# A decoder block on one core: a fourth slot for raw weights in three stages, and seven-product steps placed later in two blocks

## The chip, the core and the metric

The kernel runs on one core of one Trainium2 chip. The core has a matrix engine (PE, with its weight loads shown as PEld), VectorE (DVE), ScalarE (ACT), GpSimd (POOL) and SyncE (SP), which work through their own instruction queues and wait for one another by semaphores. Here SP issues nearly all loads of weights, and POOL issues the transfers that add to what they find in SBUF. The metric is the time of one execution on the device in microseconds (us). The kernel before takes 1745.06 us, the median of three runs (1744.52 to 1749.61).

## The reference, cut to what matters

One layer of a decoder over 256 tokens of width 2048 in float32. The weights are read once and make up nearly all of the transfers.

```python
a = rmsnorm(h, norm_mix_pre)
proj = a @ w_in                               # 2048 x 17408
q_a, k_a, v_a, q_r, f_r, i_r, g_r, gate_a, gate_r = split_columns(proj)
# attention in three dilated groups, and a gated linear recurrence (HGRN2)
y = sigmoid(gate_a) * (attn @ w_attn_branch) + sigmoid(gate_r) * (r_out @ w_hgrn_branch)
h = h + rmsnorm(y @ w_mix_out, norm_mix_post)
a = rmsnorm(h, norm_ffn_pre)
gt, up = split(a @ w_ffn_gate_up)             # 2048 x 11264
ff = (silu(gt) * up) @ w_ffn_down             # 5632 x 2048
h = h + rmsnorm(ff, norm_ffn_post)
```

## The kernel before, in words

**Products.** To keep float32 accuracy, each operand is split into a high and a low part of the type fp32r, and a product is three matmuls: high by high, high by low, low by high. ACT writes the high part of the weights (`w`, L368) and DVE the low part (`wl`, L381), both from the tile `raw` in which the float32 weights arrived.

**Blocks and steps.** The work is a list of blocks (`blocks`), each made of steps (`seq`). A block of the class `Wide` makes 1024 columns in two groups of 512 for all 256 tokens. One of its steps takes 256 rows of the weights, so 1 MB, and multiplies a 2 x 2 arrangement of tokens (two halves of 128) and rows (two of 128) by a 2 x 2 arrangement of rows and column groups. There are two kinds. An **eight-step** makes the eight products plainly, with 24 matmuls of 128 x 512. A **seven-step** makes seven products by a Strassen scheme, with 21 matmuls. For that it needs sums of weights: a transfer that POOL issues (L296) adds 256 KB to the first quarter of `raw`, once the load of that half has landed; DVE makes `sum` from `raw` (L375, L376), ACT its high part `dh` (L386) and DVE its low part `dl` (L389). It also needs sums of activations, made ahead.

**Where they stand.** Tables of strings say which step of a block is which: `EARLY` for eight blocks over `w_in` (gates, values and the recurrence's input), `FFN` for ten blocks over `w_ffn_gate_up`, `DOWN` for two over `w_ffn_down`; `MIX` for two over `w_mix_out`. Most blocks of `EARLY` and `FFN` read "87878787". In time: two narrow blocks, the early wide blocks from about 52 to 405 us, other blocks with the attention and the recurrence beside them to about 940, the mix, two narrow FFN blocks, the FFN blocks to about 1500, and the down blocks to the end.

**Slots.** The tile `raw` has `N_RAW` = 3 slots. The unit of loading is a wide step (or two narrow ones). `load_behind` is called when a step has been split, and asks for the unit three further on, whose slot is the one that the split has just read for the last time. The loads stand in SP's queue in that order, and each waits for its slot's readers.

**What stands beside a step.** While step n is being multiplied, `ahead(n)` prepares step n+2: ACT's high part, the sums where it is a seven-step, DVE's low part; and `dh` and `dl` of step n+1. `sum`, `dh` and `dl` have one buffer each, `w` and `wl` three.

**Block ends.** A wide block holds four PSUM banks (two pairs) for its outputs and four for the products that several outputs share. The next block takes them the other way round. `gather` (L451 to L454) brings the shared products into the tile `e` after the block's last seven-step: ACT copies the first (L451), DVE adds the others. `add_up` (L463) then adds the outputs. The early blocks go on with a sigmoid or a copy (L735) and a store of `e` by POOL's queue (L736); the FFN blocks with silu (L1389), a product (L1391), and a transposition on PE (L1355) inside the next block's second step. Where a block closes with a seven-step, the sums of the step after next stand ahead of the gather in DVE's queue, and its low part behind it.

**Between mix and FFN**, `from_mix_to_ffn` writes an order by hand. It splits three units early; the third has no free slot of `w` and is split into the tile `sum` (`sumslot`).

The lines that decide all this:

```python
EARLY = [order(x) for x in ["88787878"] + ["87878787"] * 6 + ["88787878"]]
FFN = [order(x) for x in ["88787878"] + ["87878787"] * 8 + ["87878787"]]
N_RAW, N_SPLIT, AHEAD, WARM, BRIDGE, LATER = 3, 3, 2, 8, 6, 16
```

Of the kernel before, what the change touches and what calls it, by code (L numbers as in the profile page):

```python
# [39 lines left out]
def order(steps):  # L40

    k = steps.count("7")
    return [(steps[:i].count(x) + k * (x == "8"), int(x == "7")) for i, x in enumerate(steps)]


EARLY = [order(x) for x in ["88787878"] + ["87878787"] * 6 + ["88787878"]]
FFN = [order(x) for x in ["88787878"] + ["87878787"] * 8 + ["87878787"]]
DOWN = [[(m, m in by7) for m in range(KF // 2)] for by7 in (range(4, 20, 3), range(3, 19, 3))]

TURN = 1  # L50
# [54 lines left out]
def tile_hybrid_block(ctx: ExitStack, tc: tile.TileContext, t, out):  # L105
# [12 lines left out]
    def nm(s):  # L118
        serial[0] += 1
        return f"{s}_{serial[0]}"  # L120
# [63 lines left out]
        )  # L184


    warm = cpool.tile([P, 512], mybir.dt.bfloat16, name="warm")
    nc.vector.memset(warm, 0.0)
    ones = cpool.tile([P, P], F32R, name="ones")
    ident = cpool.tile([P, P], F32, name="ident")  # L190
    make_identity(nc, ident)
    nc.gpsimd.tensor_scalar(ones, ident, 0.0, 1.0, op0=OP.mult, op1=OP.add)
    eps = cpool.tile([P, 2], F32, name="eps")
    nc.gpsimd.memset(eps[:, 0:1], EPS)
    nc.gpsimd.memset(eps[:, 1:2], -0.5 * EPS)
    rowg = cpool.tile([48, P], F32, name="rowg")
    nc.scalar.dma_start(rowg[0:16], t["norm_mix_pre"][0].rearrange("(a p) -> a p", p=P))
    nc.scalar.preload_act_table_set("natural_log_exp_and_others")
    colg = cpool.tile([P, 56], F32, name="colg")
    r1c = cpool.tile([P, 2], F32, name="r1c")  # L200
    rzc = cpool.tile([P, 2], F32, name="rzc")
    r2c = cpool.tile([P, 2], F32, name="r2c")
    r3c = cpool.tile([P, 2], F32, name="r3c")
    rowb = cpool.tile([P, S], F32, name="rowb")

    stage = ctx.enter_context(ExitStack())
    pool = {}

# [12 lines left out]
    kp = stage.enter_context(tc.tile_pool(name="kp", bufs=1, reuse_waits="tile"))  # L221
    enter("early")

    def fslot(s):
        return pool["now"].tile([P, 1024], F32, tag="f", bufs=16, name=nm(s))

# [9 lines left out]
    masks = {}  # L236


    blocks, seq, units = [], [], []

    def add(*args, **kw):
        b = Block(*args, **kw)
# [6 lines left out]

    def add_seven(*args, flip, whole=True, **kw):  # L250
        b = Wide(*args, **kw)
        b.flip, b.whole = flip, whole
# [23 lines left out]
    def load(u, half):  # L276

        if u >= len(units) or half >= len(units[u]):
            return
        st = units[u][half]  # L280
        b, i = st.block, st.i
        if half == 0:
            raw = stream.tile([P, 2048], F32, tag="raw", bufs=N_RAW, name=nm("raw"))
            for x in units[u]:
                x.raw = raw
        if type(b) is Wide:
            m, by7 = b.order[i]
# [12 lines left out]
        src = b.w[i * rows : (i + 1) * rows, b.col : b.col + b.width]  # L300
        src = src.rearrange("(k p) c -> p k c", p=P)
        dst = st.raw.rearrange("p (k c) -> p k c", k=b.per)
        n = len(parts(st))
        for x in range(n):
            ks = slice(x * b.per // n, (x + 1) * b.per // n)
            nc.sync.dma_start(dst[:, ks, :], src[:, ks, :])

    def load_behind(st):

        for half in (0, 1) if len(units[st.unit]) == 1 else (st.half,):  # L310
            load(st.unit + N_RAW, half)

    def wslot():
        return stream.tile([P, 2048], F32R, tag="w", bufs=N_SPLIT, name=nm("w"))

    def sumslot():
        return p3("sum", F32R, 2048, 1)

    def wlow():
        return p3("wl", F32R, 2048, 3)  # L320
# [1 line left out]
    def split(st, only=None):  # L322
# [3 lines left out]
        raw = st.raw  # L326
        if st.parts is None:
            w = (st.home or wslot)()
            st.parts = w[:, :1024], w[:, 1024:]
        wh, wl = st.parts  # L330
        for n, k in enumerate(parts(st)):
            if only in (None, n):
# [895 lines left out]
    def from_mix_to_ffn(n):  # L1228
# [4 lines left out]

        b, c, f0, f1, f2 = seq[n : n + 5]
        m = b.block
        f1.home, f2.home = wlow, sumslot
        split(f2)
        split(f0)
        load_behind(f0)
# [300 lines left out]
    mix_end = len(seq) - 2  # L1540
    w = t["w_ffn_gate_up"][0]
    add("N", w, KD, 0, lambda k: hT[0](k), evac_first_gate,
        post=more_h)
# [158 lines left out]
```

## Time and profile before

| | us |
|---|---|
| median of three runs | 1745.06 |
| the profiled execution | 1745.72 |
| its span, first to last instruction | 1743.9 |
| ACT busy, early wide blocks (353 us) | 185.8 |
| DVE idle before the first sum (L375), early wide blocks, until a load of `w_in` has landed | 37.7 |
| ACT idle before `w` (L368), FFN blocks, until a load of `w_ffn_gate_up` has landed | 101.5 |

How to read it: the page gives for each engine the time in which it worked and its share of the span. A window is a stretch of the span with each engine's busy time in it and, in brackets, how many instructions. A wait is idle time of an engine, put down to the instruction or transfer whose end released it. The chain goes back from the last instruction to what released it, step by step. In the timeline a row shows start, duration, engine, line and tiles, and in square brackets the idle time ahead of it and what ended it. Matmuls overlap in the records, so their spacing and not their duration is the rate.

### The profile page before, as it was taken

To read this page: it belongs to the slowest core of one execution; us is meant where nothing else is said; L and a number is where in the kernel's file an instruction comes from. 1 tells how busy PE (TensorE), PEld (TensorE's weight loads), DVE (VectorE), ACT (ScalarE), POOL (GpSimd) and SP (SyncE) were. 2 spreads that over 40 slices of the span, in tenths; PEclk is the share of its full clock that TensorE was granted. 3 is DMA by queue.
4 is the path that set the end of the run, shared out by engine and by line. 5 is a ranking of instruction groups with operands and counts; after the bars stand their busy time and mean duration, and the time that the engine had idled before them with its cause. 6 is when DMAs were issued, how large, how long until landed. Compare 5 with 4: busy or idle time off the path is not lost.

```text
span 1743.9 us, 21581 instructions
## 1 busy us (share of the span) xinstructions
PE 1695.9 (97%) x8220; PEld 1414.6 (81%) x8220; DVE 1416.8 (81%) x1443; ACT 914.8 (52%) x943; POOL 105.3 (6%) x141
## 2 busy tenths in 40 slices
PE   9999899999999999999999999999999999999998
PEld 7787777788888888888888888877777777888886
DVE  6888788886787987777678888888888888898887
ACT  6555455454544433544445575555555455665663
POOL 0111110111000000000000000000000000000000
PEclk9999999999999999999999999999999999999999
DMA  8787777778554655465458747776777777777663
GB/s 284 220 255 239 219 239 240 234 229 282 188 165 161 206 181 181 158 217 172 155 179 262 253 129 240 224 208 202 213 210 215 213 207 209 225 236 227 209 211 124
DMA packets 218600, 367.07 MB, mean 210 GB/s; under 512 B 12064, under 2 KB 78672, under 8 KB 218496
## 3 DMA queue, kind: packets, MB, share of 16 engines
q1 hardware_dynamic: 198208, 317.89, 55.2%
q0 software_dynamic: 17664, 41.89, 11.4%
q10 hardware_dynamic: 2624, 5.92, 1.0%
q8 instruction: 64, 1.05, 0.2%
q14 instruction: 40, 0.33, 0.1%
HBM read 354.12 MB, written 11.53 MB: 210 GB/s over the span
## 4 chain that ended last, share of the span: by engine, by line
PE 54%; DMA 16%; DVE 10%; issue 3%; ACT 2%; POOLq 0%; DVEq 0%; SPq 0%; ACTq 0%
PE acc L164 39%; PE aux L164 14%; DMA raw<-in_w_ffn_gate_up 12%; DVE wl L381 4%; DMA raw<-in_w_in 4%; ACT w L368 1%; DVE e L463 1%; DVE dl L389 1%; DVE e L454 1%; DVE sum L376 1%; DVE e L1391 0%; DVE e L452 0%; PE aux L889 0%; DVE e L453 0%; DVE sum L375 0%
## 5 line engine op out<-in xcount | busy, mean ns | idle before, releaser
L368 ACT ACTIVATE w<-raw 128x2048 fp32r<-128x2048 f32 x204 | 390.1, 1912 | 360.7 <-DMA raw<-in_w_ffn_gate_up 103.3
L381 DVE TENSOR_TENSOR wl<-raw,w 128x2048 fp32r<-128x2048 f32 x204 | 466.5, 2287 | 31.1 <-ACT w L368 28.1
L164 PE MATMUL acc<-xT,w 128*128 128x256 f32 (+1 forms) x2048 | 369.8, 339 | 0.0
L164 PEld LDWEIGHTS acc<-xT,w 128*128 128x128 f32 x2048 | 312.0, 188 | 43.8
L334 DVE TENSOR_TENSOR w<-raw,w 128x1024 fp32r<-128x1024 f32 (+1 forms) x191 | 232.5, 1218 | 133.0 <-ACT w L333 131.9
L333 ACT ACTIVATE w<-raw 128x1024 fp32r<-128x1024 f32 (+1 forms) x191 | 200.8, 1053 | 224.5 <-PE acc L164 179.4
L386 ACT ACTIVATE dh<-sum 128x1536 fp32r<-128x1536 f32 x85 | 126.5, 1488 | 92.5 <-DVE sum L376 67.3
L164 PE MATMUL acc<-w,hT 128*128 128x512 f32 x566 | 170.1, 392 | 5.0 <-DVE e L452 5.0
L164 PE MATMUL acc<-w,xT 128*128 128x512 f32 x524 | 157.2, 397 | 7.2 <-DVE e L452 6.9
L389 DVE TENSOR_TENSOR dl<-sum,dh 128x1536 fp32r<-128x1536 f32 x85 | 148.9, 1752 | 3.0 <-ACT dh L386 3.0
L375 DVE TENSOR_TENSOR sum<-raw 128x512 f32<-128x512 f32 x85 | 58.5, 688 | 114.1 <-issue 44.1
L164 PE MATMUL aux<-w,hT 128*128 128x512 f32 x414 | 137.8, 397 | 8.7 <-DVE e L452 8.7
L164 PEld LDWEIGHTS acc<-w,hT 128*128 128x128 f32 x566 | 105.7, 188 | 28.5 <-DVE e L452 6.7
L164 PEld LDWEIGHTS acc<-w,xT 128*128 128x128 f32 x524 | 98.8, 190 | 29.5 <-DVE e L452 7.8
L164 PE MATMUL aux<-w,xT 128*128 128x512 f32 x332 | 110.4, 398 | 6.6 <-DVE e L452 6.6
L376 DVE TENSOR_TENSOR sum<-raw,sum 128x1024 f32<-128x1024 f32 x85 | 104.1, 1225 | 2.9
L164 PEld LDWEIGHTS aux<-w,hT 128*128 128x128 f32 x414 | 79.2, 191 | 27.1 <-DVE e L452 10.4
L164 PE MATMUL aux<-w,a 128*128 128x512 f32 x280 | 88.6, 389 | 0.0
L164 PE MATMUL acc<-w,a 128*128 128x512 f32 x280 | 88.3, 389 | 0.0
L164 PE MATMUL acc<-wl,hT 128*128 128x512 f32 x211 | 81.3, 393 | 3.6 <-DVE wl L381 3.6
L164 PE MATMUL aux<-wl,hT 128*128 128x512 f32 x207 | 82.0, 396 | 1.5 <-DVE wl L381 1.5
L164 PEld LDWEIGHTS aux<-w,xT 128*128 128x128 f32 x332 | 63.7, 192 | 21.2 <-DVE e L452 7.8
(284 smaller groups left out, 2620.2 us busy)
## 6 DMA issues: line engine op xcount, KB each, us to landing
raw<-in_w_in SPq DMA_DIRECT2D x271, 512.0 KB, 4.7
raw<-in_w_ffn_gate_up SPq DMA_DIRECT2D x176, 512.0 KB, 4.7
raw<-in_w_ffn_down SPq DMA_DIRECT2D x88, 512.0 KB, 5.1
raw<-in_w_mix_out SPq DMA_DIRECT2D x32, 512.0 KB, 5.6
raw<-in_w_ffn_gate_up POOLq DMA_DIRECT2D x39, 256.0 KB, 4.4
kept<-e POOLq DMA_DIRECT2D x16, 512.0 KB, 4.9
raw<-in_w_hgrn_branch SPq DMA_DIRECT2D x16, 512.0 KB, 4.4
raw<-in_w_attn_branch SPq DMA_DIRECT2D x16, 512.0 KB, 4.4
```

The costliest lines, as they stand in the source:

```text
L164: nc.tensor.matmul(ps, lhsT, rhs, start=start, stop=stop, skip_group_check=True)
L333: nc.scalar.activation(wh[:, k], raw[:, k], AF.Copy)
L334: nc.vector.tensor_sub(wl[:, k], raw[:, k], wh[:, k].bitcast(F32))
L368: nc.scalar.activation(hi, raw, AF.Copy)
L375: nc.vector.tensor_sub(d[:, 0], w[:, 0], w[:, 2])
L376: nc.vector.tensor_sub(d[:, 1:], w[:, 1:4:2], d[:, 0:1].to_broadcast([P, 2, 512]))
L381: nc.vector.tensor_sub(lo, raw, hi.bitcast(F32))
L386: nc.scalar.activation(hi, flat, AF.Copy)
L389: nc.vector.tensor_sub(lo, flat, hi.bitcast(F32))
L454: nc.vector.tensor_sub(e[:, 2:], e[:, 0:4:3], x["p7"][:, None, :].to_broadcast([P, 2, 512]))
L463: nc.vector.tensor_add(e, b.bank[keys], e)
```

## The change

It has two parts and what makes room for them.

1. **A fourth slot.** A new tile `raw` with one buffer is taken from the pool of the stage (`p3`), beside the three slots of the pool `stream`. Lists of units in `extra` say which units use it: every fourth one, from the fourth of the early wide blocks to the last of them, and again from the fifth unit of the FFN wide blocks to the end. While such a list runs, `load_behind` asks for the unit four further on instead of three; where a list begins, it asks for one unit more, and where it ends, it asks for none.
2. **Steps placed later.** The first early block reads "88878878" instead of "88787878": two seven-steps instead of three, the fourth and the seventh step. The first FFN block reads "88878787": three as before, the fourth, sixth and eighth step, so that it closes with one.
3. **Room.** The small tile `rowg` moves to the pool of the early stage, which is opened earlier in the program for it, and the third unit between mix and FFN is split into the tiles `dh` and `dl` instead of `sum`, which shrinks from 2048 to 1536 elements a partition.

```diff
-EARLY = [order(x) for x in ["88787878"] + ["87878787"] * 6 + ["88787878"]]
-FFN = [order(x) for x in ["88787878"] + ["87878787"] * 8 + ["87878787"]]
+EARLY = [order(x) for x in ["88878878"] + ["87878787"] * 6 + ["88787878"]]
+FFN = [order(x) for x in ["88878787"] + ["87878787"] * 8 + ["87878787"]]
...
-    rowg = cpool.tile([48, P], F32, name="rowg")
+    rowg = pool["now"].tile([48, P], F32, name="rowg")
...
-            raw = stream.tile([P, 2048], F32, tag="raw", bufs=N_RAW, name=nm("raw"))
+            raw = raw_slot(u)
...
+    def raw_slot(u):
+        if any(u in x for x in extra):
+            return p3("raw", F32, 2048, 1)
+        return stream.tile([P, 2048], F32, tag="raw", bufs=N_RAW, name=nm("raw"))
+
     def load_behind(st):
 
-        for half in (0, 1) if len(units[st.unit]) == 1 else (st.half,):
-            load(st.unit + N_RAW, half)
+        u, depth, more = st.unit, N_RAW, None
+        for x in extra:
+            if u == x[0] - N_RAW - 1:
+                more = x[0]
+            if x[0] - N_RAW <= u < x[-1]:
+                depth = N_RAW + 1
+            elif u == x[-1]:
+                return
+        for half in (0, 1) if len(units[u]) == 1 else (st.half,):
+            load(u + depth, half)
+            if more:
+                load(more, half)
...
-    def sumslot():
-        return p3("sum", F32R, 2048, 1)
+    def sums_home():
+        return [p3(x, F32R, 1536, 1)[:, :1024] for x in ("dh", "dl")]
...
-            st.parts = w[:, :1024], w[:, 1024:]
+            st.parts = w if type(w) is list else (w[:, :1024], w[:, 1024:])
...
-        f1.home, f2.home = wlow, sumslot
+        f1.home, f2.home = wlow, sums_home
...
+    wide = [st.unit for st in seq if type(st.block) is Wide]
+    extra.append(range(wide[0] + N_RAW, wide[0] + 64, N_RAW + 1))
+    first = blocks[mix_last + 3].unit0 + N_RAW + 1
+    extra.append(range(first, len(units) + N_RAW + 1, N_RAW + 1))
```

How it moves instructions, at three places. First POOL's queue at the end of the first and of the second early block. `raw` with its numbers is a unit's tile of weights, `kept<-e` the store of a block's result. Before:

```order
L296 DMA raw_139_850<-in_w_in 128x512
L736 DMA kept_145_914<-e_140_875 128x1024 x2
L296 DMA raw_150_929<-in_w_in 128x512
L296 DMA raw_163_1000<-in_w_in 128x512
L296 DMA raw_172_1067<-in_w_in 128x512
L296 DMA raw_181_1138<-in_w_in 128x512
L736 DMA kept_186_1198<-e_185_1193 128x1024 x2
```

and with the change:

```order
L296 DMA raw_142_885<-in_w_in 128x512
L751 DMA kept_143_913<-e_138_873 128x1024 x2
L296 DMA raw_154_964<-in_w_in 128x512
L296 DMA raw_165_1033<-in_w_in 128x512
L296 DMA raw_174_1104<-in_w_in 128x512
L296 DMA raw_185_1200<-in_w_in 128x512
L751 DMA kept_184_1196<-e_183_1191 128x1024 x2
```

Four adding transfers lie between two pairs of stores in both. But the last one ahead of the second pair, `raw_181`, belongs to the fourth step of the third block, and `raw_185` to that block's sixth: the transfer for the sixth step has moved ahead of the stores of the block before.

Second, DVE's queue in the first early block. `wl` is the low part of a step's weights, `sum` and `dl` belong to a seven-step; `f`, `s` and `so` are sums of activations, `g` a gate of the block before. Before, from the second step's `wl` on:

```order
L381 TENSOR_TENSOR wl_588<-raw_468,w_587 128x2048
L479 TENSOR_TENSOR so_562<-s_563,so_562 128x512
L375 TENSOR_TENSOR sum_619<-raw_525 128x512
L376 TENSOR_TENSOR sum_619<-raw_525,sum_619 128x1024
L381 TENSOR_TENSOR wl_617<-raw_525,w_616 128x2048
L486 TENSOR_TENSOR f_656<-xT_109 128x512
L473 TENSOR_TENSOR s_659<-f_656 128x256
L474 TENSOR_TENSOR s_659<-s_659,f_656 128x128
L475 TENSOR_TENSOR s_659<-f_656,s_659 128x128
L389 TENSOR_TENSOR dl_664<-sum_619,dh_663 128x1536
L381 TENSOR_TENSOR wl_667<-raw_571,w_666 128x2048
```

and with the change:

```order
L396 TENSOR_TENSOR wl_591<-raw_468,w_590 128x2048
L494 TENSOR_TENSOR so_565<-s_566,so_565 128x512
L396 TENSOR_TENSOR wl_619<-raw_525,w_618 128x2048
L501 TENSOR_TENSOR f_656<-xT_109 128x512
L488 TENSOR_TENSOR s_659<-f_656 128x256
L489 TENSOR_TENSOR s_659<-s_659,f_656 128x128
L490 TENSOR_TENSOR s_659<-f_656,s_659 128x128
L390 TENSOR_TENSOR sum_666<-raw_528 128x512
L391 TENSOR_TENSOR sum_666<-raw_528,sum_666 128x1024
L396 TENSOR_TENSOR wl_664<-raw_528,w_663 128x2048
```

The two sums have moved from the third step's weights (`raw_525`) to the fourth's (`raw_528`), behind the sums of activations, and one set of `sum` and `dl` less stands in the block.

Third, DVE's queue at the end of the first FFN block, around its gather (into `e`). Before:

```order
L389 TENSOR_TENSOR dl_8628<-sum_8598,dh_8627 128x1536
L381 TENSOR_TENSOR wl_8631<-raw_8534,w_8630 128x2048
L381 TENSOR_TENSOR wl_8663<-raw_8568,w_8662 128x2048
L452 TENSOR_TENSOR e_8691<-acc_8543,e_8691 128x512
L453 TENSOR_TENSOR e_8691<-acc_8550,e_8691 128x512
L454 TENSOR_TENSOR e_8691<-e_8691,acc_8550 128x1024
L375 TENSOR_TENSOR sum_8699<-raw_8602 128x512
L376 TENSOR_TENSOR sum_8699<-raw_8602,sum_8699 128x1024
L381 TENSOR_TENSOR wl_8697<-raw_8602,w_8696 128x2048
L463 TENSOR_TENSOR e_8691<-aux_8450,e_8691 128x1024
```

and with the change:

```order
L404 TENSOR_TENSOR dl_8659<-sum_8629,dh_8658 128x1536
L396 TENSOR_TENSOR wl_8662<-raw_8530,w_8661 128x2048
L390 TENSOR_TENSOR sum_8696<-raw_8564 128x512
L391 TENSOR_TENSOR sum_8696<-raw_8564,sum_8696 128x1024
L467 TENSOR_TENSOR e_8720<-acc_8574,e_8720 128x512
L468 TENSOR_TENSOR e_8720<-acc_8581,e_8720 128x512
L469 TENSOR_TENSOR e_8720<-e_8720,acc_8581 128x1024
L478 TENSOR_TENSOR e_8720<-aux_8446,e_8720 128x1024
L478 TENSOR_TENSOR e_8720<-aux_8459,e_8720 128x1024
L396 TENSOR_TENSOR wl_8694<-raw_8564,w_8693 128x2048
```

The sums for the next block's second step now stand ahead of the gather, and that step's `wl` behind both adds of L463 (L478 in the changed file), as at the ends of the other FFN blocks.

More of the change, by code (lines that the diff above doesn't have):

```diff
@@ L184, in rsqrt_mean @@
         )
[L187 to L195, printed above, removed]
-    rowg = cpool.tile([48, P], F32, name="rowg")
[L197 to L204, printed above, removed]
     stage = ctx.enter_context(ExitStack())
@@ L222, in tile_hybrid_block @@
     enter("early")
+    warm = cpool.tile([P, 512], mybir.dt.bfloat16, name="warm")
+    nc.vector.memset(warm, 0.0)
+    ones = cpool.tile([P, P], F32R, name="ones")
+    ident = cpool.tile([P, P], F32, name="ident")
+    make_identity(nc, ident)
+    nc.gpsimd.tensor_scalar(ones, ident, 0.0, 1.0, op0=OP.mult, op1=OP.add)
+    eps = cpool.tile([P, 2], F32, name="eps")
+    nc.gpsimd.memset(eps[:, 0:1], EPS)
+    nc.gpsimd.memset(eps[:, 1:2], -0.5 * EPS)
+    rowg = pool["now"].tile([48, P], F32, name="rowg")
+    nc.scalar.dma_start(rowg[0:16], t["norm_mix_pre"][0].rearrange("(a p) -> a p", p=P))
+    nc.scalar.preload_act_table_set("natural_log_exp_and_others")
+    colg = cpool.tile([P, 56], F32, name="colg")
+    r1c = cpool.tile([P, 2], F32, name="r1c")
+    rzc = cpool.tile([P, 2], F32, name="rzc")
+    r2c = cpool.tile([P, 2], F32, name="r2c")
+    r3c = cpool.tile([P, 2], F32, name="r3c")
+    rowb = cpool.tile([P, S], F32, name="rowb")
     def fslot(s):
@@ L236, in tile_hybrid_block @@
     masks = {}
-    blocks, seq, units = [], [], []
+    blocks, seq, units, extra = [], [], [], []
     def add(*args, **kw):
@@ L251, in add_seven @@
         b = Wide(*args, **kw)
-        b.flip, b.whole = flip, whole
+        b.flip, b.whole, b.unit0 = flip, whole, len(units)
         blocks.append(b)
@@ L1540, in tile_hybrid_block @@
     mix_end = len(seq) - 2
+    mix_last = len(blocks) - 1
     w = t["w_ffn_gate_up"][0]
```

## The prediction

> **What bounds the kernel now.** The page first: the matrix engine (PE) has work 97% of the span, yet only about half of the chain that ended last is PE; the rest is transfers and VectorE (DVE).
>
> ```profile
> span 1743.9 us, 21581 instructions
> ...
> PE 1695.9 (97%) x8220; PEld 1414.6 (81%) x8220; DVE 1416.8 (81%) x1443; ACT 914.8 (52%) x943; POOL 105.3 (6%) x141
> ...
> PE 54%; DMA 16%; DVE 10%; issue 3%; ACT 2%; POOLq 0%; DVEq 0%; SPq 0%; ACTq 0%
> ```
>
> A busy share averages over stages, so next the windows: the early wide blocks (52 to 405 us), the FFN wide blocks (1100 to 1500), the down blocks (1503 to 1700), and one stretch of 50 us. Behind PE's busy time stand its instructions in brackets; the last three columns are the granted PE clock, the share of the transfer engines and GB/s.
>
> ```profile
> 52.00:405.00 353.00, 333.99 (x1433) 271.75 (x1433) 291.65 (x208) 185.77 (x122) 35.43 (x47) 0.98 0.77 235
> 1100.00:1500.00 400.00, 381.11 (x1684) 310.14 (x1683) 339.04 (x231) 213.76 (x146) 29.90 (x35) 0.99 0.72 210
> 1503.00:1700.00 197.00, 197.00 (x875) 163.26 (x874) 175.13 (x166) 119.12 (x110) 10.27 (x12) 1.00 0.71 220
> ...
> 1100.00:1150.00 50.00, 48.14 (x210) 39.37 (x209) 41.44 (x29) 28.46 (x21) 4.25 (x5) 0.97 0.68 195
> ```
>
> The down blocks never wait. The chain gives their undisturbed rate, and the timeline the length of a group of eight transposes:
>
> ```profile
> 1529.90 12.92 PE aux L164 x57
> ...
> 1108.25 1.03 PE L1355 MATMUL aux<-ident,e 128*128 128x128 f32 x8
> ```
>
> 12.92/57 = 0.2267 us a product. An eight-step (24 matmuls) is then 5.44 us and a seven-step (21) 4.76. The lost time of a stage is its length less its instructions at this rate. Early: 353 - 1433 x 0.2267 = **28.2 us**. FFN: nine groups of transposes (72 instructions, 9 x 1.03 = 9.3 us) are among the 1684; 400 - 1612 x 0.2267 - 9.3 = **25.3 us**. Control: the down stretch gives 197 - 875 x 0.2267 = -1.4, so the method is good to 1%. Together 53.5 us are lost in the two stages, and nothing that the change touches is lost elsewhere.
>
> Whom PE waits for, early and then FFN:
>
> ```profile
> PE acc L164 <- DVE e L452: 6.9, 2, 5.2
> PE aux L164 <- DVE e L452: 6.6, 3, 3.4
> PE acc L164 <- DVE wl L381: 2.2, 2, 1.5
> PE acc L164 <- DVE dl L389: 1.7, 2, 1.0
> PE aux L164 <- DVE wl L381: 1.6, 3, 0.8
> ...
> PE aux L164 <- DVE e L452: 8.7, 4, 2.8
> PE acc L164 <- DVE e L452: 5.0, 4, 1.6
> PE acc L164 <- DVE wl L381: 3.6, 5, 0.8
> PE aux L164 <- DVE wl L381: 1.5, 2, 0.7
> ```
>
> 19.0 and 18.8 us of waits, mostly for L452, the add that empties the PSUM pair a block left behind; the next block's first product needs that pair. The rest of the 53.5 is restart after a wait and the clock: the 50 us stretch above holds one wait of 50 - 48.14 = 1.9 us and a mean granted clock of 0.97, which is 1.5 us more. The Trainium skill ("TensorE: Matmul & The Clock Gate", Part 1) has the clock fall only after a whole idle window of about 3.4 us; the trace disagrees, since it fell around 1.9. By that page the FFN would lose little beyond its 18.8 of waits, and some 6 us less could be won; the measurement decides.
>
> Why is L452 late? The chain around one such boundary:
>
> ```profile
> 1128.92 1.42 DVE wl L381
> ...
> 1130.36 3.91 DMA raw<-in_w_ffn_gate_up
> ...
> 1135.09 6.10 DMA raw<-in_w_ffn_gate_up
> ...
> 1141.33 1.92 ACT w L368
> ...
> 1143.76 0.70 DVE e L452
> ```
>
> The last reader of a raw slot (wl, L381) ends at 1130.34; the load goes into it; a seven-step's adding transfer on POOL's queue (L296) may start only when that has landed; at 1141.18 the unit is whole. That is **10.8 us from free slot to usable weights**. ScalarE's (ACT) split and DVE's sums stand ahead of L452 in their queues, so L452 waits for weights that are not its own. DVE around it:
>
> ```profile
> 1141.27 0.69 DVE L375 TENSOR_TENSOR sum<-raw 128x512 f32<-128x512 f32 x1 [3.00 <-DMA raw<-in_w_ffn_gate_up]
> 1141.99 1.23 DVE L376 TENSOR_TENSOR sum<-raw,sum 128x1024 f32<-128x1024 f32 x1
> 1143.76 0.69 DVE L452 TENSOR_TENSOR e<-aux,e 128x512 f32<-128x512 f32 x1 [0.55 <-ACT e L451]
> ...
> 1145.29 1.22 DVE L454 TENSOR_TENSOR e<-e,aux 128x1024 f32<-128x1024 f32 x1
> 1146.61 2.35 DVE L463 TENSOR_TENSOR e<-acc,e 128x1024 f32<-128x1024 f32 x2
> 1148.88 2.28 DVE L381 TENSOR_TENSOR wl<-raw,w 128x2048 fp32r<-128x2048 f32 x1
> 1151.08 1.22 DVE L1391 TENSOR_TENSOR e<-e 128x1024 f32<-128x1024 f32 x1
> 1152.22 1.75 DVE L389 TENSOR_TENSOR dl<-sum,dh 128x1536 fp32r<-128x1536 f32 x1
> ...
> 1188.85 0.69 DVE L452 TENSOR_TENSOR e<-acc,e 128x512 f32<-128x512 f32 x1 [0.55 <-ACT e L451]
> ```
>
> DVE's only large idle time in the FFN is at L375 (two rows), and early it is the same place (third row):
>
> ```profile
> DVE sum L375 <- issue: 30.9, 10, 5.0
> DVE sum L375 <- DMA raw<-in_w_ffn_gate_up: 19.6, 7, 3.7
> ...
> DVE sum L375 <- DMA raw<-in_w_in: 37.7, 10, 5.3
> ```
>
> **The fourth slot.** With three slots, unit u+3 is loaded once u is split. Between that wl and the sums of u+3 DVE itself runs sums (1.9), wl (2.2), dl (1.7), wl (2.2): 8.0 us, start to start from the rows above. The weights take 10.8: 2.8 short, and the row of L375 shows 3.00. With four slots u+4 is loaded, a seven-step's load follows a seven-step's wl, and at PE's pace there lie two pairs of steps less one sums-and-wl: 2 x (5.44 + 4.76) - 4.1 = 16.3 us. The shortage of 2.8 becomes a reserve of **5.5**. Then the waits at L375 go, and with them the cause of the L452 waits.
>
> What is late next? DVE's own work: per FFN block 4 x 8.0 for the steps plus 2.8 (gather, L452 to L454), 2.3 (L463) and 1.1 (L1391) is 38.2 us against PE's 4 x (5.44 + 4.76) + 1.0 = 41.8. It fits, at 91%. At the boundary, counted from the start T of a closing seven-step with weights in time: ACT's split waits for PE's step before and ends at T+2.1, the copy L451 takes 0.55 (the wait in L452's row), L452 runs T+2.65 to T+3.35, and PE wants its pair at T+4.76: 1.4 us early. The wl of step 1 ends 7.4 us after L452 starts (1143.76 to 1151.16 above), at T+10.05; PE wants it at T+4.76+5.44+0.23 = T+10.43. That margin is only 0.4 us, dl's about 0.5. So each boundary costs between 0 and half of the present 25.3/9 = 2.8 us, that is 1.4. I take **0.3**, near the lower end since each margin comes out positive: with 16 boundaries 4.8 us stay.
>
> Queues: the extra load ahead of the first early wide block waits for no slot, and ahead of the second FFN step only for users of earlier stages; each later load stands in SP's order where a load stood. POOL's adding transfer of a block's sixth step now stands ahead of the two stores of the block before (L736). It waits for its load, so the stores go out at about T+15 (step 1's wl at T+10.05 and one landing) and no longer soon after L463's end at T+7.9: at most 7 us later. Behind the stores only the next adding transfers wait, and the tile e is next written a block later, 41 us off. So 0; without those 41 us of cover it would be the 7 us once per early block.
>
> **The steps placed later.** The first early block has two seven-steps instead of three: 24 - 21 = 3 more matmuls, 3 x 0.2267 = **+0.7 us** on PE. Its two dl waits (1.7 us above) should go, being part of the 28.2; the wait of at most 0.8 us for the first wl stays, since DVE there still works on the block before. The first FFN block keeps three, shifted by one, and now closes with one, which makes its boundary like the others (counted in the 16). There PE waited for nothing, so the bounds are 0 and 1.4; I take the 0.3 included. Splitting the third unit between stages into dh and dl instead of sum has the same two instructions; the ACT write already follows a split waiting for the same PE step: 0. Moving rowg and the fourth slot behind the down blocks: PE never waits there, 0.
>
> **Sum**, against the profiled execution's 1745.72 us (span 1743.9 and 1.8 around it; the median shown is 1745.06, 0.7 less): 1745.7 - 53.5 + 0.8 + 4.8 + 0.7 = 1698.5; from the median 1697.8. I say **1698**.
>
> **Rivals.** *Transfers become the bound early.* The stretch at 235 GB/s moved 353 x 235 = 83 MB; in 353 - 28.2 + 5 = 330 us that is 252 GB/s.
>
> ```profile
> GB/s 284 220 255 239 219 239 240 234 229 282 188 165 161 206 181 181 158 217 172 155 179 262 253 129 240 224 208 202 213 210 215 213 207 209 225 236 227 209 211 124
> ...
> 400.00:450.00 50.00, 48.64 (x265) 41.98 (x266) 34.55 (x39) 25.11 (x30) 6.05 (x9) 1.00 0.82 267
> ...
> raw<-in_w_in SPq DMA_DIRECT2D x120, 512.0 KB, 5.4
> raw<-in_w_in POOLq DMA_DIRECT2D x29, 256.0 KB, 4.3
> ...
> raw<-in_w_ffn_gate_up SPq DMA_DIRECT2D x128, 512.0 KB, 4.8
> ```
>
> For it: few slices exceed 252. Against it: 50 us at 267 and a slice at 284 exist, and the share would be 0.77 x 252/235 = 0.83, as in that window. If half the early loss stays: 14.1 instead of about 3, hence 1709. Chance 0.13.
>
> *DVE becomes the bound at the boundaries.* The margins of 0.4 and 0.5 us may be negative. At 1.4 instead of 0.3 a boundary: 16 x 1.1 = 17.6 more, 1716. For it: DVE at 91% with an in-order queue; against it: the worked times. Chance 0.16.
>
> *It doesn't reach the cause.* If POOL's transfer stays late for another reason than the slot, DVE waits as now: 1746. The chain, in which slot, load and transfer follow without a gap, speaks against. Chance 0.05.
>
> *Slower.* The adding transfer shares 16 engines with deeper loads in front. If a full chain grows from 10.8 beyond 16.3 + 2.8 = 19.1 us, DVE waits longer than now. The waits at L375 (50.5 us in the FFN) cost PE about half of themselves (25.3); at 20.0 us the 27 late units of the three rows x 0.9 x 0.5 = 12 us more: 1759. Against it: a load's landing rises only from 4.8 us in the FFN, at a share of 0.72, to 5.4 early, at 0.77. The Trainium skill ("DMA: Bandwidth & Descriptors", Queues, rings and completion order) says that each engine goes round the queues that have work, packet by packet; by that rule a deeper load queue can't starve POOL's transfer, and this rival falls. No run here shows it. Chance 0.04.
>
> **How the numbers follow.** The forecast (1690 to 1705) has 0.60; the two halves 0.16 and 0.13, none 0.05, slower 0.04, and 0.02 for better than 1690, more than all that is lost. The range runs from 1690 (every boundary free and the rate's 1% in favour) to 1718 (the boundary rival, 1716, with the same 0.3% around). It leaves out about 0.15. A measurement here tells 0.3%, 5.2 us, from no change. Faster by more than that: 0.60 + 0.16 + 0.13 + 0.02 = 0.91; same 0.05; slower 0.04.
>
> **What would show it.** L375 without waits in both stages; PE's waits for the add of L452 gone, windows of 50 us with 50 us busy, about 220 matmuls and clock 1.00; block to block 41.8 us in the FFN instead of 45.1 (L452 at 1143.76, 1188.85); early transfers near 250 GB/s; three matmuls more. Wrong would be: L375 still waiting for raw (transfers), or waits for wl and dl of about a microsecond after each boundary with L375 prompt (DVE).

## The result, and the profile after

| | before | after |
|---|---|---|
| median of four runs each, us | 1744.79 | 1694.26 |
| lowest to highest, us | 1741.20 to 1749.61 | 1693.67 to 1695.53 |
| profiled execution, us | 1745.72 | 1694.15 |
| its span, us | 1743.9 | 1692.4 |

The ratio is 0.971, with a 95% interval from 0.9685 to 0.9734. The forecast was 1698, between 1690 and 1718. In the profiled execution 51.6 us are saved where the sum had 47.2.

The changed file has 15 lines more ahead of the helpers, so the lines of before that are named here are found 15 further on (L296 stays): the first sum is L390 (L375), `wl` L396 (L381), `dl` L404 (L389), the first add of the gather L467 (L452), the adds of outputs L478 (L463).

The page of after first: engine busy times, and the chain's shares by engine.

```profile
span 1692.4 us, 21514 instructions
...
PE 1680.6 (99%) x8223; PEld 1410.5 (83%) x8223; DVE 1413.2 (84%) x1440; ACT 912.8 (54%) x942; POOL 104.2 (6%) x140
...
PE 93%; DMA 2%; DVE 2%; issue 1%; ACT 1%; SPq 0%; DVEq 0%; ACTq 0%
```

PE has gone from 97% to 99% busy, but the chain tells more: 93% of it is PE instead of 54%, and transfers and DVE together 4% instead of 26%. Three matmuls more stand in it, as the change of the first early block says.

The windows of after: early wide blocks; 1080 to 1480 us, which are the FFN blocks up to 1451 and the start of the down blocks; and 50 us of the early stage (behind PE, PEld, DVE, ACT and POOL stand the granted PE clock, the share of the transfer engines and GB/s).

```profile
52.00:385.00 333.00, 331.43 (x1460) 273.31 (x1459) 294.97 (x212) 185.38 (x123) 34.51 (x46) 1.00 0.80 253
1080.00:1480.00 400.00, 400.00 (x1805) 330.96 (x1804) 361.84 (x253) 228.25 (x161) 30.79 (x36) 1.00 0.75 229
200.00:250.00 50.00, 50.00 (x222) 41.40 (x221) 43.89 (x29) 27.43 (x18) 5.70 (x8) 1.00 0.86 275
```

In the FFN window PE is busy for 400 us of 400; before it was 381.11. In the early blocks 333 - 1460 x 0.2267 = 2.0 us are lost where 28.2 were. The clock is 1.00 in all of them, and early transfers run at 253 GB/s. DVE works 361.84 of 400 us in the FFN window, 90%.

All that PE waits for DVE in the whole of after, the longest first:

```profile
PE aux L164 <- DVE warm L206: 1.2, 1, 1.2
PE aux L164 <- DVE wl L396: 0.6, 1, 0.6
PE acc L164 <- DVE wl L396: 0.6, 1, 0.6
PE acc L164 <- DVE dl L404: 0.3, 1, 0.3
PE acc L164 <- DVE w L349: 0.2, 1, 0.2
```

There is no row for the gather (L467) any more; before, L452 alone had 27.2 us in the two stages. `warm` stands at the program's start. What DVE waits for, early (two rows) and in the FFN (one row):

```profile
DVE sum L390 <- DMA raw<-in_w_in: 18.5, 7, 3.6
DVE dl L404 <- ACT dh L401: 8.1, 8, 2.0
...
DVE dl L404 <- ACT dh L401: 25.2, 18, 2.0
```

In the FFN the wait at the sums is gone and DVE's spare time has moved to `dl`, where it waits for ACT and PE doesn't wait for it. Early, 18.5 us of waits at the sums are still there; before there were 50.9, the 37.7 until a load had landed and 13.2 for which the profile shows no releaser. PE doesn't feel what is left.

An FFN boundary in after, first on DVE, then the chain on PE (start, duration, instructions):

```profile
1115.30 0.69 DVE L467 TENSOR_TENSOR e<-aux,e 128x512 f32<-128x512 f32 x1 [0.40 <-ACT e L466]
...
1157.07 0.69 DVE L467 TENSOR_TENSOR e<-acc,e 128x512 f32<-128x512 f32 x1 [0.40 <-ACT e L466]
...
1162.19 2.29 DVE L396 TENSOR_TENSOR wl<-raw,w 128x2048 fp32r<-128x2048 f32 x1
```

```profile
1154.55 2.72 PE acc L164 x12
1157.27 2.04 PE aux L164 x9
1159.31 6.80 PE acc L164 x30
```

The closing seven-step is the 12 + 9 matmuls from T = 1154.55, and the next block takes its pair at 1159.31. L467 ends at 1157.76, 1.55 us before that (forecast: 1.4). The `wl` of the next block's second step ends at 1164.48; PE needs it at 1159.31 + 5.44 + 0.23 = 1164.98, so 0.5 us remain (forecast: 0.4). From gather to gather it is 1157.07 - 1115.30 = 41.77 us, where 41.8 was forecast and 45.1 stood before.

### The profile page after: what moved, and what is told of

The parts are those of the page before. It is cut to its first block, busy times and chain, and to the rows that moved or that the text cites. A ratio compares the mean times of both kernels' runs of the same rounds, so it can differ in the third digit from the quotient of the medians.

```text
span 1692.4 us, 21514 instructions
## 1 busy us (share of the span) xinstructions
PE 1680.6 (99%) x8223; PEld 1410.5 (83%) x8223; DVE 1413.2 (84%) x1440; ACT 912.8 (54%) x942; POOL 104.2 (6%) x140
## 4 chain that ended last, share of the span: by engine, by line
PE 93%; DMA 2%; DVE 2%; issue 1%; ACT 1%; SPq 0%; DVEq 0%; ACTq 0%
PE acc L164 60%; PE aux L164 32%; DMA raw<-in_w_in 2%; DVE wl L396 1%; PE aux L904 0%; PE acc L1370 0%; DVE fz L1492 0%; PE aux L573 0%; PE aux L1370 0%; ACT w L383 0%; DVE w L349 0%; DVE dl L404 0%; PE aux L561 0%; ACT junk L1447 0%; DVE e L1443 0%
## 5 line engine op out<-in xcount | busy, mean ns | idle before, releaser
L396 DVE TENSOR_TENSOR wl<-raw,w 128x2048 fp32r<-128x2048 f32 x204 | 466.5, 2287 | 34.6 <-ACT w L383 32.0
L404 DVE TENSOR_TENSOR dl<-sum,dh 128x1536 fp32r<-128x1536 f32 x84 | 147.3, 1753 | 37.7 <-ACT dh L401 37.6
L390 DVE TENSOR_TENSOR sum<-raw 128x512 f32<-128x512 f32 x84 | 57.5, 684 | 25.9 <-DMA raw<-in_w_in 18.5
```

What stands on the lines that cost most here:

```text
L390: nc.vector.tensor_sub(d[:, 0], w[:, 0], w[:, 2])
L396: nc.vector.tensor_sub(lo, raw, hi.bitcast(F32))
L404: nc.vector.tensor_sub(lo, flat, hi.bitcast(F32))
```

## The experiments

Three questions: which part of the change brings the time; whether it is the slot as such, or that the weights are usable in time; and how much reserve there is now. Each kernel's time is a median, with the lowest and highest run; the ratio is to the kernel before, run on the same chip.

### Which part: slot_only, order_only, slot_early, slot_ffn

`slot_only` is after with the old tables, `order_only` is before with the new ones:

```diff
-EARLY = [order(x) for x in ["88878878"] + ["87878787"] * 6 + ["88787878"]]
-FFN = [order(x) for x in ["88878787"] + ["87878787"] * 8 + ["87878787"]]
+EARLY = [order(x) for x in ["88787878"] + ["87878787"] * 6 + ["88787878"]]
+FFN = [order(x) for x in ["88787878"] + ["87878787"] * 8 + ["87878787"]]
```

`slot_early` and `slot_ffn` are after without the one or the other list of units:

```diff
 # slot_early
-    extra.append(range(first, len(units) + N_RAW + 1, N_RAW + 1))
 # slot_ffn
-    extra.append(range(wide[0] + N_RAW, wide[0] + 64, N_RAW + 1))
```

slot_only: 

> The fourth slot alone, both first wide blocks with their old order of steps. If the slot carries the gain: 1693 to 1697 us (one seven-step more in the first early block saves 0.7 us on PE, and up to 1.7 us of waits for dl and about 0.5 for a first sum may come back). If the later placement carries a good part of it: 1700 us or more, with PE waiting in the first early block (52 to 100 us) or around the end of the first FFN block.

order_only: 

> The later placement alone, three slots everywhere. If the slot carries the gain: 1742 to 1747 us, PE's waits for the add of the gather as before. If the placement carries a good part: 1738 us or less.

slot_early: 

> The fourth slot in the early wide blocks only (both placements new). If the two stages lose their time apart, early 28.2 us and FFN 25.3: 1715 to 1721 us, with the FFN stretch losing what it lost before. If the early stage is held by its transfers and not by the slot, the gain here would be under 15 us: 1730 or more.

slot_ffn: 

> The fourth slot from the FFN wide blocks to the end only (both placements new). By the two losses: 1718 to 1724 us, early waits as before; the gains of this run and of the early one add up to that of the whole change within 3 us. If a common cause (a clock that recovers, transfers that spread) joins the stages, they don't add up.

The kernel before took 1746.19 us beside these four.

| kernel | us | lowest to highest | ratio, 95% |
|---|---|---|---|
| slot_only | 1697.06 | 1696.90 to 1698.53 | 0.9725, 0.9705 to 0.9746 |
| order_only | 1737.08 | 1731.97 to 1742.19 | 0.9950, 0.9931 to 0.9969 |
| slot_early | 1721.34 | 1718.70 to 1722.49 | 0.9861, 0.9839 to 0.9882 |
| slot_ffn | 1712.01 | 1709.94 to 1716.90 | 0.9818, 0.9788 to 0.9847 |

The slot alone brings 49.1 us, nearly all, and lands at the upper end of what was expected of it. The new places alone bring 9.1, so order_only fell under "the placement carries a good part". Both can't be added: together the two bring 50.5, so on top of the slot the places are worth only 1.4 to 2.8 us by these medians, and the two intervals overlap. slot_early is 0.3 us above its range, slot_ffn 6 below. Their gains on before, 24.9 and 34.2, don't add up to that of the whole change, since the places' 9.1 are in both. Counted from order_only, the early list is worth 1737.08 - 1721.34 = 15.7 us and the FFN list 1737.08 - 1712.01 = 25.1: together 40.8, and after lies 42.8 below order_only. order_only itself scatters over 10 us, so each of these is good to a few us only. The windows from 1080 to 1480 us, of slot_early and then of slot_ffn, say the same without that scatter: the FFN loses what it lost before without its list, and nothing with it.

```profile
1080.00:1480.00 400.00, 380.96 (x1680) 309.97 (x1679) 339.44 (x233) 212.73 (x145) 29.09 (x34) 0.99 0.72 212
1080.00:1480.00 400.00, 400.00 (x1800) 330.73 (x1800) 363.64 (x251) 227.15 (x158) 30.81 (x37) 1.00 0.76 227
```

Where the 9.1 us of order_only come from, in its windows (early, FFN):

```profile
52.00:405.00 353.00, 336.98 (x1472) 274.60 (x1471) 296.03 (x214) 186.31 (x124) 34.65 (x46) 1.00 0.78 239
1100.00:1500.00 400.00, 381.60 (x1687) 310.85 (x1686) 340.63 (x234) 213.72 (x147) 28.77 (x34) 0.99 0.73 214
```

and in what PE waits for there, early:

```profile
PE aux L164 <- DVE e L452: 7.1, 3, 2.4
PE acc L164 <- DVE e L452: 4.2, 2, 2.3
PE aux L164 <- DVE wl L381: 2.9, 4, 0.8
PE acc L164 <- DVE wl L381: 1.8, 3, 0.8
```

1472 matmuls instead of 1433 in the same 353 us are 39 x 0.2267 = 8.8 us, and the FFN has not moved (1687 for 1684). So it is the early table. Its waits sum to 16.0 us instead of 19.0 (the rows for `dl` are gone), but the longest for the gather is 2.4 us instead of 5.2, and the clock is 1.00 instead of 0.98. That would be some 7 us of 353, about the 6 that the waits leave open. How much of it belongs to the places is not shown: the mean clock of a whole execution differs from run to run, 0.991 to 0.996 in before and 0.993 to 0.997 in order_only. Why moving one block's steps shortens the gather waits of later blocks was not taken further. slot_ffn fell below its expected 1718 to 1724 for the same reason: early it has 1482 matmuls in the same 353 us, so 17 us were left to lose there, not 28.

### The slot or the latency: no_add

Before, with its three slots, but without POOL's adding transfer:

```diff
-                    nc.gpsimd.dma_start(raw[:, :512], rows, accum_op=OP.add)
+                    pass
```

> Three slots and the old placement, with the adding transfers on POOL's queue left out (the sums of weights are then wrong; everything else is computed). If the time from a free slot to usable weights is what binds: it falls from 10.8 us to about 5.5, under the 8.0 us that DVE gives it, so DVE stops waiting at the first sum and PE's waits go with three slots too: 1692 to 1702 us. If three slots hold too few loads in flight whatever their latency: 1715 or more.

It took 1692.00 us (1691.74 to 1692.07), ratio 0.9702 (0.9685 to 0.9719). What PE waits for DVE is as little as in after, with three slots:

```profile
PE aux L164 <- DVE warm L188: 1.2, 1, 1.2
PE aux L164 <- DVE wl L381: 0.6, 1, 0.6
PE acc L164 <- DVE w L334: 0.2, 1, 0.2
```

So three slots are enough once the weights are usable after the load alone. Leaving the transfer out also takes its bytes off the engines, and the loads themselves land a little sooner (a median of 4.8 us early instead of 5.4); that this alone would do is ruled out further down, where transfers of 8 KB bring most of the loss back. The loss sat in the time from a free slot to usable weights, of which the adding transfer is the second half; a fourth slot hides it, and doing without it removes it. That the kernel is then at 1692.0 and after at 1694.3 also says how little the change leaves: of these 2.3 us, 0.7 are the three matmuls that after has more.

### How much reserve: late2_after, late4_after, late2_before

The forecast gave the fourth slot a reserve of 5.5 us. To spend it, the adding transfer was made later by multiplying a piece of the weights by 1.0 on POOL, twice or four times, in after; and twice in before:

```diff
+                    for _ in range(2):
+                        nc.gpsimd.tensor_scalar(raw[:, :1024], raw[:, :1024], 1.0, None, op0=OP.mult)
                     nc.gpsimd.dma_start(raw[:, :512], rows, accum_op=OP.add)
```

late2_after: 

> The whole change, with two multiplications by 1.0 of the first half of raw on POOL ahead of each adding transfer: about 4.5 us more from free slot to usable weights (the trace will give the number). If four slots leave a reserve of about 5.5 us there: 1694 to 1702 us. If the reserve is mostly used up by queueing or only the steady steps have it: 1715 or more.

late4_after: 

> The same with four multiplications, about 9 us more: 10.8 + 9 = 19.8 against 16.3, short by 3.5 us as the kernel before was by 2.8. By the reserve: DVE waits at the first sum again and the time is back at 1735 to 1765 us. If the slots are not what matters: under 1710.

late2_before: 

> The kernel before with two multiplications (about 4.5 us more): 15.3 against 8.0, short by 7.3 us for two seven-steps a block. A block is then 38.2 us of DVE work and 2 x 7.3 of waits, some 53 us instead of 45: 17 blocks give 1845 to 1900 us. If latency is not what binds: under 1780.

None came out as the reserve would have it: 1832.39 us (ratio 1.0518, 1.0489 to 1.0546), 2224.29 (1.2754, 1.2719 to 1.2789) and 2015.54 (1.1557, 1.1526 to 1.1588). The first lies under "1715 or more", but not by that argument, and the other two lie above both of their ranges. The groups of late2_after show why they don't measure the reserve; first POOL's new line in the whole run, then DVE's `dl` between 1100 and 1500 us (busy, mean ns of one, idle before):

```profile
L297 POOL TENSOR_SCALAR raw<-raw 128x1024 f32<-128x1024 f32 x168 | 566.0, 3369 | 573.7 <-DMA raw<-in_w_ffn_gate_up 142.6 <-DMA raw<-in_w_mix_out 136.2 <-DMA raw<-in_w_ffn_down 113.0
...
L406 DVE TENSOR_TENSOR dl<-sum,dh 128x1536 fp32r<-128x1536 f32 x33 | 71.2, 2156 | 0.0
```

One multiplication takes 3.37 us in the mean, so two delay by 6.7, more than the whole assumed reserve; and while POOL multiplies, DVE's own work is stretched: the same `dl` takes 1752 ns in before.

```profile
L389 DVE TENSOR_TENSOR dl<-sum,dh 128x1536 fp32r<-128x1536 f32 x36 | 63.1, 1752 | 1.1 <-ACT dh L386 1.1
```

The Trainium skill ("SBUF — State Buffer", SBUF: two separate sides) states that a VectorE instruction with two inputs in SBUF and a GpSimd instruction that reads SBUF lock each other out of a shared pair of ports; the 2156 ns agree with it in direction. A cleaner delay was needed.

### How much reserve, with transfers alone: hop1, hop3

A small reload of 16 columns that are already there, on POOL's queue, once or three times ahead of each adding transfer of after. It moves 8 KB and uses no engine's time beside the issue.

```diff
+                    again = b.w[2 * m * P : (2 * m + 1) * P, col : col + 16]
+                    nc.gpsimd.dma_start(raw[:, :16], again)
                     nc.gpsimd.dma_start(raw[:, :512], rows, accum_op=OP.add)
```

hop1: 

> The whole change, with one small transfer more on POOL's queue ahead of each adding transfer: 16 columns of the same weights are loaded again, after the load and before the adding one (the result is the same). It lengthens the way from free slot to usable weights by one landing and one issue, an estimated 3 us from a store of 64 KB that lands in 1.6 us plus POOL's 0.9 and its semaphores, and leaves DVE alone. If four slots leave about 5.5 us: no more than 1694 to 1698 us. If the reserve isn't there: 1715 or more.

hop3: 

> The same with three such transfers, an estimated 9 us more: 10.8 + 9 = 19.8 against 16.3, short by 3.5 us. By the reserve DVE waits at the first sum again and the time is back at 1735 to 1765 us. If the slots' count and not the latency matters: under 1705.

hop1 took 1736.97 us (1723.95 to 1745.29 in ten runs; ratio 0.9963, 0.9938 to 0.9989): the reserve isn't there. hop3 took 2011.46 (ratio 1.1526, 1.1490 to 1.1562), far above both of its ranges. The size of the delay, first in two rows of POOL's timeline of hop1 (L298 is the reload, L299 the adding transfer), then as the reload's median time to landing, early and in the FFN:

```profile
1131.26 0.55 POOL L298 DMA_DIRECT2D raw<-in_w_ffn_gate_up  x1 [1.62 <-DMA raw<-in_w_ffn_gate_up]
1133.77 0.87 POOL L299 DMA_DIRECT2D raw<-in_w_ffn_gate_up  x1 [1.95 <-DMA raw<-in_w_ffn_gate_up]
...
raw<-in_w_in POOLq DMA_DIRECT2D x29, 8.0 KB, 4.9
...
raw<-in_w_ffn_gate_up POOLq DMA_DIRECT2D x36, 8.0 KB, 3.7
```

From reload to adding transfer it is 2.5 us in these rows, but between 2.3 and 6.3 over the FFN, with a median of 4.4, and between 2.4 and 9.8 early, with a median of 5.2. So in the FFN nearly all of the delays are under 5.5, and early more than a third are over it. PE waits again, 22.4 us for DVE's `wl`, `dl` and gather in all, and most of it early (the profiled execution is the fastest of the ten, so this understates it). The two largest rows, then the windows, early and FFN:

```profile
PE aux L164 <- DVE wl L399: 7.9, 8, 1.8
PE acc L164 <- DVE e L470: 4.8, 3, 3.6
...
52.00:405.00 353.00, 338.77 (x1474) 274.59 (x1474) 295.89 (x214) 186.76 (x125) 51.02 (x76) 1.00 0.79 241
1080.00:1480.00 400.00, 396.06 (x1773) 326.56 (x1772) 359.15 (x246) 224.52 (x154) 51.93 (x73) 1.00 0.77 225
```

So a reserve of 5.5 us at every step is not there. In after itself it can be read step by step. Here are the fourth to eighth steps of one FFN block: POOL's adding transfers for the fourth, sixth and eighth step, then DVE's sums and the `wl` that frees the fourth step's slot. The eighth step's weights go into that same slot.

```profile
1154.30 0.88 POOL L296 DMA_DIRECT2D raw<-in_w_ffn_gate_up  x1 [7.62 <-DMA raw<-in_w_ffn_gate_up]
1168.89 0.85 POOL L296 DMA_DIRECT2D raw<-in_w_ffn_gate_up  x1 [13.71 <-ACT act L1376]
1178.80 0.85 POOL L296 DMA_DIRECT2D raw<-in_w_ffn_gate_up  x1 [9.06 <-DMA raw<-in_w_ffn_gate_up]
...
1169.39 0.68 DVE L390 TENSOR_TENSOR sum<-raw 128x512 f32<-128x512 f32 x1
1171.25 2.28 DVE L396 TENSOR_TENSOR wl<-raw,w 128x2048 fp32r<-128x2048 f32 x1
1177.32 0.68 DVE L390 TENSOR_TENSOR sum<-raw 128x512 f32<-128x512 f32 x1
1184.09 2.29 DVE L396 TENSOR_TENSOR wl<-raw,w 128x2048 fp32r<-128x2048 f32 x1
1186.50 0.69 DVE L390 TENSOR_TENSOR sum<-raw 128x512 f32<-128x512 f32 x1
```

The view of POOL's transfers of `raw` by tile gives their time to landing: 4.9 us for the fourth step's, 4.5 for the sixth's, and for the eighth's

```profile
DMA to landing us min/median/max: 7.6/7.6/7.6
```

So the fourth step's weights are usable at 1159.2, 10.2 us before DVE comes to them; the sixth's 3.9 us before; the eighth's at 1186.4, **0.1 us before**. That 0.1 is not a reserve: DVE is done with its work before it at 1186.38 and starts as soon as the weights have landed. Worked out in this way over the FFN blocks of after, the fourth step has 7.3 to 12.3 us to spare and the eighth 0.1 to 2.1. In the early blocks from the third on the fourth step has 6.3 to 9.2, the sixth 0.1 to 0.7, and at the eighth DVE waits for the weights, 2.6 to 3.6 us in each block, as here:

```profile
210.44 0.69 DVE L390 TENSOR_TENSOR sum<-raw 128x512 f32<-128x512 f32 x1 [2.59 <-DMA raw<-in_w_in]
```

The same place may be behind hop3's size: its three reloads delay the adding transfer by some 10 us (medians of 11.3 early and 10.2 in the FFN), and a step with nothing to spare is then short by about 10 and not by 3.5. That was not taken apart.

### The same delay where there is reserve: hop_loose

If that is so, the reload of hop1 must cost nothing ahead of a fourth step:

```diff
+                    if i == 3 and m == 1:
+                        again = b.w[2 * m * P : (2 * m + 1) * P, col : col + 16]
+                        nc.gpsimd.dma_start(raw[:, :16], again)
                     nc.gpsimd.dma_start(raw[:, :512], rows, accum_op=OP.add)
```

> The kernel after, with the small reload of hop1 (16 columns, some 2.5 to 3.9 us more between load and adding transfer) only ahead of the adding transfers of the fourth step of those wide blocks of the early and FFN stages that read 87878787 (6 and 9 of them, and the mix where a fourth step is of that form). In the trace of after the adding transfer of such a step has landed 6.3 to 9.2 us (early, from the third block on) and 7.3 to 12.3 us (FFN) before VectorE comes to the sums; of an eighth step 0.1 us early and 0.1 to 2.1 us in the FFN. Theory (the reserve is that of each place in the block: none at the eighth step, whose slot the late fourth step of the same block frees, and much at the fourth): the delay is swallowed, 1693 to 1697 us, and PE waits as little as in after (under 5 us in all). Rival (the reloads cost the same wherever they stand, by POOL's queue or by the engines they take): hop1 lost 42.7 us with 84 of them, 0.5 us each, so 15 of them give about 7.6 us and 1702.

It took 1693.94 us (1693.07 to 1694.84 in six runs), ratio 0.9703 (0.9679 to 0.9726), the time of after. The reload is there. The adding transfer behind it starts 2.3 us after it in these rows, 2.3 to 5.0 us over the FFN and 4.6 to 5.5 early:

```profile
1153.65 0.57 POOL L298 DMA_DIRECT2D raw<-in_w_ffn_gate_up  x1 [8.19 <-DMA raw<-in_w_ffn_gate_up]
1155.98 0.86 POOL L299 DMA_DIRECT2D raw<-in_w_ffn_gate_up  x1 [1.76 <-DMA raw<-in_w_ffn_gate_up]
```

A price per reload wherever it stands would have given 1702. The reserve belongs to the place in the block. It also says that the reload costs nothing by itself, so what hop1 lost is the delay.

### What the freed time allows: more7

In after PE is the bound in these stages, so fewer matmuls should now be fewer microseconds. The first early block and each down block got one seven-step more in place of an eight-step, and some of their seven-steps moved:

```diff
-EARLY = [order(x) for x in ["88878878"] + ["87878787"] * 6 + ["88787878"]]
+EARLY = [order(x) for x in ["88878787"] + ["87878787"] * 6 + ["88787878"]]
...
-DOWN = [[(m, m in by7) for m in range(KF // 2)] for by7 in (range(4, 20, 3), range(3, 19, 3))]
+DOWN = [[(m, m in by7) for m in range(KF // 2)] for by7 in ((4, 7, 9, 11, 13, 16, 19), (3, 6, 8, 10, 12, 15, 18))]
```

> The whole change with a seven-step more in the first early block (the fourth, sixth and eighth step) and in each down block (seven instead of six). PE has 9 matmuls fewer, 2.0 us. DVE has 3.7 us more in the early block and an estimated 5.3 in each down block (sums of weights 1.9, dl 1.75, sums of activations 1.7), so 93 of 98 us there. If DVE keeps up: 1691 to 1693.5 us, 0.999 of the changed kernel. If it doesn't: 1694.5 or more, with waits for wl or the gather in the down blocks.

It took 1692.82 us (1691.61 to 1694.74 in five runs), ratio 0.9710 (0.9686 to 0.9735). Its span in the profiled execution is 1689.8 us against 1692.4: nine matmuls less at 0.2267 are 2.0, and no new wait stands against them (0.6 us for `wl` is all beside the start). By the medians it is 1.4 us below after, by the ratios not to be told apart.

## Why the prediction was right, and where it was not

**The bound and the lost time: right.** 53.5 us were said to be lost in two stages, and nothing elsewhere. After, 2.0 are lost early and none in the FFN. The parts agree, within order_only's scatter: slot_ffn lies 25.1 us below order_only, against 25.3 lost in the FFN; places and early slot together bring 9.1 + 15.7 = 24.8 early, against the 28.2 - 0.8 - 0.7 = 26.7 that the sum had there without its boundaries.

**What stands behind the waits: right.** The time lost beyond the 18.8 us of FFN waits was taken for restart and clock, and counted as won. None of it is lost after. In before the granted clock stood at 0.50 for 3.41 us twice in the FFN, right behind waits of 1.86 and 1.96 us:

```profile
1144.60:1148.01 3.41, 3.41 (x8) 2.66 (x9) 3.27 (x4) 2.44 (x3) 0.58 (x1) 0.50 0.57 76
1325.51:1328.92 3.41, 3.41 (x9) 2.65 (x8) 3.31 (x4) 2.04 (x3) 0.00 (x0) 0.50 0.25 44
```

Half of twice 3.41 is 3.4 us; the other 3.1 of the 6.5 are left for restarts, which no run splits further. By the Trainium skill's rule ("TensorE: Matmul & The Clock Gate", Part 1), a clock that falls only after an idle window of about 3.4 us, these two drops would not be there; the trace decides against it here.

**The cause, a late adding transfer behind a late slot: right.** no_add takes away the transfer and keeps three slots, and lands at 1692.0; hop1 delays it with four slots, by a reload of 8 KB each, and loses 42.7 us of the gain; hop_loose does so where there is time to spare and loses nothing. The rival that the change doesn't reach the cause is gone with the result itself.

**The boundaries: mis-sized.** The sum kept 16 x 0.3 = 4.8 us. The margins behind it were right at the boundary shown, 1.55 us measured for 1.4 and 0.5 for 0.4, and a margin that is positive costs nothing: PE waits once for 0.6 us in the early blocks past the first, and never in the FFN. The 0.3 was a value between bounds where the working had already given the lower one. This is nearly all of the 4.4 us by which the profiled execution came out below the sum. The 0.7 for three matmuls stands by the count of 8223, and the 0.8 for the first block lies inside the 2.0 us: PE waits there for `wl` and `dl`, 0.9 us in all.

**The reserve of 5.5 us: wrong, without a price.** The step that failed is "2 x (5.44 + 4.76) - 4.1 = 16.3 us". It takes the mean spacing of steps for the spacing of each. On DVE the fourth step's sums come late, behind the gather and the adds of the block before, and the eighth's don't. From 1169.39 to 1186.50 are 17.1 us and not 20.4; and from the end of `wl` at 1173.53 to the sums are 13.0 us and not 16.3. Nor do the weights take 10.8 there: from 1173.53 to 1186.4 are 12.9, of which 7.6 are the adding transfer. 13.0 less 12.9 is the 0.1 that the trace shows, and early the shortage is still there at the eighth step. The time came out right because PE needed no reserve, and that four slots are just enough is luck: nothing in the working says it, and delays that are mostly smaller than the 5.5 take most of the gain away.

**L375 without waits in both stages: half right.** In the FFN they are gone; early 18.5 us remain, for the same reason. PE isn't late by them. The likely reason, not tested: DVE's work and these waits together are 294.97 + 18.5 = 313.5 of 333 us, where before they were 291.65 + 50.9 = 342.6 of 353.

**The rivals.** Early transfers ran at 253 GB/s over the stage and at 275 in one stretch of 50 us, so 252 was no ceiling. DVE at 90% in the FFN did not become the bound. The one on the slower side, an adding transfer slowed by deeper loads, had its direction right. The transfers of before and then of after in windows of the two stages (early, FFN):

```profile
raw<-in_w_in POOLq DMA_DIRECT2D x29, 256.0 KB, 4.3
...
raw<-in_w_ffn_gate_up POOLq DMA_DIRECT2D x35, 256.0 KB, 4.4
```

```profile
raw<-in_w_in POOLq DMA_DIRECT2D x29, 256.0 KB, 6.1
...
raw<-in_w_ffn_gate_up POOLq DMA_DIRECT2D x34, 256.0 KB, 5.6
```

Its median landing grew by 1.8 and 1.2 us, far from the 8.3 (10.8 to 19.1) that this rival needed at the least. The Trainium skill ("DMA: Bandwidth & Descriptors", Queues, rings and completion order) has engines go round the queues that have work, and that agrees with a transfer that is slowed and not starved.

**POOL's stores up to 7 us later: harmless**, as said; no wait for a store or for `e` on its way out appears in PE's rows. **The steps placed later** were taken as +0.7 and the two waits for `dl`; alone they bring 9.1 us, of which 3.0 are waits in the profiled execution and much of the rest may be the clock. That doesn't show in the total, since the slot takes the same loss away.

## What to carry to other kernels

When a buffer is added, compare the time from a free slot to usable data with the shortest interval between a slot's last reader and its next, place by place over a block, and not with the mean: here the mean said 5.5 us to spare and the tightest place had none. Where the engine that waits at the end has become fully busy, a positive margin costs nothing, so put it at nothing in the sum and give the chance that it is negative to a rival. A tiny extra transfer in a queue is a cheap probe for such a reserve, and putting it at one place only tells where it is.

## What was not expected of the hardware

- Deeper loads stretch the adding transfers (4.3 to 6.1 us early) more than the loads themselves, whose median went from 5.4 to 5.5 us early (4.8 to 5.1 in the FFN, where the adding ones went from 4.4 to 5.6).
- POOL's multiplication of 128 x 1024 float32 took 3.37 us in the mean, and stretched DVE's `dl` by 23% (1752 to 2156 ns).
- The granted clock fell to 0.50 for 3.41 us behind waits of under 2 us.
- The kernels in which PE waits scatter. hop1 ran over 21 us, and the clock goes with it: 1723.95 us at a mean of 0.998, 1745.29 at 0.993. before ran from 1738.43 to 1753.62 beside hop_loose. after, no_add and hop_loose, in which PE hardly waits, stay within 2 us at 0.998 to 0.999.
